# A two-layer trunk of convolution and attention on one NeuronCore: adding loads of half a weight piece, two woven projection blocks, an earlier turn

## The chip, the cores and the metric

The kernel runs on one core of a Trainium2 chip. The metric is the device time of one execution in microseconds; smaller is better. Before the change three runs took 1907.27 to 1909.2 us, with a median of 1909.15 us.

## The reference

Two layers work on 256 tokens of 2048 channels in float32. What matters of a layer:

```python
h = rmsnorm(x, norm_g)
proj = h @ w_in          # c_a, c_glu, c_gate, q_down, kv_down, k_pe, m_gate, g_conv, g_mla
...
y_conv = conv_branch(c_a, c_glu, c_gate, ...) @ w_proj_conv
y_mla = mla_branch(q_down, kv_down, k_pe, m_gate, ...) @ w_proj_mla
y = jax.nn.sigmoid(g_conv) * y_conv + jax.nn.sigmoid(g_mla) * y_mla
return x + y @ w_out
```

The conv branch is a gated unit, a causal depthwise convolution of width 31, a layer norm over the channels, a swish and a gate. The other branch is multi-head latent attention.

## The kernel before

**Products.** All weights stream from HBM once for each layer. A weight matrix is cut into blocks of 512 columns, and a block into pieces of two K tiles (`KS = 2`): 128 partitions by 2 x 512 columns, 512 KB. The projections with 2048 inputs (`gmla`, `gconv`, `pmla`, `pconv`, `wout` among them) have eight pieces to a block. To keep float32 accuracy each operand is split in two: `hi`, rounded to the type in which TensorE works, and `lo`, the remainder. A piece gives 12 matmuls: for two halves of the tokens and two K tiles, `hi` weights with the `hi` and the `lo` of the stationary side, and `lo` weights with its `hi`. One piece of one block is one tick of the program's clock; the text calls it a slot too.

**Splitting.** `split_hi` makes `hi` on ScalarE (ACT), `split_lo` makes `lo = raw - hi` on VectorE (DVE). `prepare`, called ahead of each unit's matmuls, splits `hi` three units ahead and `lo` two; both have four buffers. For the pieces listed in `ADDED_BY_DMA` DVE does nothing: ACT writes `lo = -hi` for both K tiles, and a DMA on the GpSimd (POOL) queue adds the raw weights to it from HBM. These are pieces 1 and 5 of the blocks of `gmla`, `gconv`, `pmla` and of the first two of `pconv` (where the first two pieces of a block are replaced, as told next, only piece 5).

**Seven in place of eight.** `gconv`, `wout` and the second half of `pconv` run as pairs of blocks (`SEVEN`). The first two pieces of both blocks of a pair are replaced by seven products of a quarter each (`q1` to `q7`, six matmuls each) on sums of weights and of activations. `q1`, `q7`, `q6` and `q5` stand in the tail of the block before (`TAIL`, counted from its end), the other three at the front of the pair. DVE forms the sums of weights (`sum`), `make_forms` those of the stationary side (`form_a`, `form_b`).

**Order.** `InOrder` keeps the instructions of each engine in the order in which the program writes them. Steps are put down for a slot to come (`at_slot`). What is left of DVE's time in a slot by `background`'s costs is filled from a queue, `fill`: first the taps of the convolution, then the layer norm and the gating (`layernorm`). The last step of these, `separated`, writes a quarter of `ycT` (512 channels), hi on ACT and lo on DVE. `pconv` reads it: pieces 0 and 1 use the first quarter, 2 and 3 the second, 4 and 5 the third, 6 and 7 the last. `before_pconv` puts in whatever is still missing of a quarter when a piece needs it.

**Turning.** An evacuated tile of `y` (or of the next layer's `h`) is turned by way of HBM: `park` writes it there in four DMAs, `fetch` reads it back after `fetch_at` slots, and after `at` slots DVE transposes within blocks of 32. `turn4` sets these numbers for each quarter `c`.

Every recorded operation has the line of `InOrder`'s helper, 132 (133 in the changed kernel), so instructions are known by their tiles: `acc`, `left`, `right` are PSUM accumulators, `tap` and `v_t` belong to the convolution, `turned` to a turn.

Of the kernel before, what the change touches and what calls it, by code (L numbers as in the profile page):

```python
# [11 lines left out]
F32 = mybir.dt.float32  # L12
# [108 lines left out]
def trunk(ctx: ExitStack, tc: tile.TileContext, xT, x, g_in, pos, win, wuq, wukv, wpc, wpm, wo, cst, rows, invf, out):  # L121
# [67 lines left out]

    TAIL = {8: (-7, -5, -3, -2), 12: (-7, -5, -3, -2)}  # L190

    def plan_all():
        blocks = [(l, k, i, pieces_of(l, s)) for l in range(DEPTH) for k, i, s in order_of_layer()]
        seven, home = None, 0
        for at, (l, k, i, block) in enumerate(blocks):
            first = (l, k, i) in SEVEN
            if at > 0 and blocks[at - 1][:3] in SEVEN:
                continue
# [8 lines left out]
            after = at + 1 + first  # L207
            following = blocks[after] if after < len(blocks) else None
# [76 lines left out]
    def split_hi(i):  # L285
        if i >= len(units) or i in highs:
            return
        load(i)
        form(i)
        n = units[i].n  # L290
        paired = n == PAIRED
        both = split_p.tile([P, KS, 2 * n if paired else n], F32R, tag="hi", name=f"hi{i}", bufs=4)
        highs[i] = both[:, :, :n]
        if paired:
            pairs_of[i] = both
        singly = i < N_SINGLE
        if i == 0:
            one = [slice(a, a + 1) for a in range(KS)]
            scale_x(0, "hi", vec)
            scale_x(0, "lo", vec)  # L300
            act.copy(highs[i][:, one[0]], full(i)[:, one[0]])
            scale_x(1, "hi", vec)
            act.copy(highs[i][:, one[1]], full(i)[:, one[1]])
            split_lo(i, one[0])
            scale_x(1, "lo", vec)
            split_lo(i, one[1])
        for a in () if i == 0 else range(0, KS, 1 if singly else KS):
            k = slice(a, a + 1 if singly else KS)

            if singly:  # L310
                act.copy(highs[i][:, k], full(i)[:, k])
            for c in range(min(i * KS + k.start, NCT), min(i * KS + k.stop, NCT)):
                scale_x(c, "hi", act)
                scale_x(c, "lo", vec)
            if singly:
                split_lo(i, k)
            else:
                act.copy(highs[i][:, k], full(i)[:, k])
        if units[i].added:
            lo = split_p.tile([P, KS, n], F32R, tag="lo", name=f"lo{i}", bufs=4)  # L320
            act.activation(lo, highs[i].bitcast(F32), AF.Copy, scale=-1.0)
            gps.dma_start(lo, sources[units[i].source][0], accum_op=ALU.add)
            done[i] = highs[i], lo, KS
        for a in range(1, LOAD_AHEAD + 1):
            load(i + a)

    def split_lo(i, k=slice(0, KS)):
        if i >= len(units) or done.get(i, (0, 0, 0))[2] >= k.stop:
            return
        n = units[i].n  # L330
        if i in pairs_of:
            lo = pairs_of[i][:, :, n:]
# [3 lines left out]
        done[i] = highs[i], lo, k.stop  # L336

# [27 lines left out]
    def background(n, more):  # L365
# [186 lines left out]
    def product(planned, stat, evacuate, evac_at=EVAC_AT, costs=(0.0, 0.0), before=None, tardy=None, closing=None):  # L552
# [4 lines left out]
        else:  # L557
            dst = [accumulators(f"acc{planned.pieces[0]}")]

        def evac(right, ts=range(T)):  # L560
            for t in ts:
                evacuate(*((right,) if seven else ()), t, dst[right][t][:, : 2 * n] if n == PAIRED else dst[right][t][:, :n])

# [6 lines left out]
        for at, tick in enumerate(planned.ticks):  # L570
# [16 lines left out]
            for t, kk, part in [(t, kk, p) for t in range(T) for p in range(2) for kk in range(KS)] if n == PAIRED else ():  # L587
# [4 lines left out]
                )  # L592
            for t, kk, part in () if n == PAIRED else order_of_products(i, final, j == tardy):
                k = j * KS + kk
# [6 lines left out]
                )  # L601
            if final and planned.begins:
                half = tuple(c / 2 for c in costs)
# [208 lines left out]
    for l in range(DEPTH):  # L812
# [711 lines left out]
        def evac_of(f, i, pl):  # L1524
            return (lambda b, t, ps: f(i + b, t, ps)) if pl.seven else (lambda t, ps: f(i, t, ps))

# [5 lines left out]
        for at_block, (kind, i, pl) in enumerate(planned):  # L1532
# [5 lines left out]
            def stage_behind(b):  # L1538
                return planned[b + 1 + bool(planned[b][2].seven)][0]

# [3 lines left out]

            of, after = pl.begins, at_block + 1 + bool(pl.seven)
            if of:
# [59 lines left out]
            elif kind == "pconv":  # L1606
                while "yc" not in keep:
                    run_fill()
                product(pl, stat_of(*keep["yc"]), evac_of(pconv_evac, i, pl), 0 if i + bool(pl.seven) == 3 else EVAC_AT, (2.4, 0.0),
                        before=before_pconv if i == 0 else None)  # L1610
# [118 lines left out]
```

## Time and profile before

| | |
|---|---|
| median of three runs | 1909.15 us |
| the profiled execution | 1904.81 us |
| its span, first to last instruction | 1903.0 us |
| mean granted TensorE clock | 0.995 |
| busy: TensorE, VectorE, ScalarE, GpSimd | 1874.6, 1664.4, 1407.1, 538.3 us |
| moved by DMA | 475.45 MB, 250 GB/s |

The views used are the page, the waits of an engine, the groups of instructions by form, the DMA issues, the timeline of one engine, and sums over stretches of time. In the waits a row names who waited, for what, and the microseconds in total, the number of times and the longest. In a timeline row stand the start, the length, the instructions, and in brackets the idle time before with what ended it. The gate stages (`gmla`, `gconv`) lie at about 500 to 685 us in the first layer and 1450 to 1630 in the second, `pmla` behind them, then `pconv` at about 778 to 835 and 1722 to 1785.

### The profile page before, as it was taken

How to read it: one execution, taken by the hardware profiler on the slowest of the kernel's cores; microseconds unless marked ns; L12 is line 12 of the kernel's file. 1: busy time of each engine (PE TensorE's matmuls, PEld its weight loads, DVE VectorE, ACT ScalarE, POOL GpSimd, SP SyncE). 2: the span in 40 equal slices, each digit the busy share in tenths (PEclk: the TensorE clock that was granted, in tenths of full speed). 3: DMA queues.
4: the chain of work that ended last, by engine and by line, in shares of the span. 5: the costliest groups of instructions: out<-in, count | busy, mean ns of one | idle time of the engine just before them, and what ended most of it. 6: DMA issues, size and time to landing. Idle time of an engine off the chain costs nothing. (4 is left out here: it accounts for less than half of the span.)

```text
span 1903.0 us, 26913 instructions
## 1 busy us (share of the span) xinstructions
PE 1874.6 (99%) x8389; PEld 1550.1 (81%) x8389; DVE 1664.4 (87%) x2618; ACT 1407.1 (74%) x2461; POOL 538.3 (28%) x990
## 2 busy tenths in 40 slices
PE   9999999999998999999999999999999989999999
PEld 8888888888877788788888888888887877887887
DVE  6998988889998898979869989888899988888895
ACT  6678888888886685755657689888899866776553
POOL 0155555532200000121421545555322000111211
PEclk9999999999999999999999999999999999999999
DMA  8777777787877689778976777787778867888785
GB/s 319 226 264 262 261 258 247 264 258 245 261 222 208 209 234 265 238 248 257 339 259 212 266 260 257 252 259 260 248 249 266 231 204 220 261 250 254 238 267 199
DMA packets 147312, 475.45 MB, mean 250 GB/s; under 512 B 24608, under 2 KB 29984, under 8 KB 147168
## 3 DMA queue, kind: packets, MB, share of 16 engines
q1 hardware_dynamic: 106416, 364.74, 57.7%
q0 software_dynamic: 39744, 107.79, 20.5%
q8 instruction: 66, 1.08, 0.2%
q10 hardware_dynamic: 1008, 1.20, 0.2%
q14 instruction: 78, 0.64, 0.1%
HBM read 429.59 MB, written 44.04 MB: 249 GB/s over the span
## 5 line engine op out<-in xcount | busy, mean ns | idle before, releaser
L132 ACT CAST hi<-raw 128x1024 fp32r<-128x1024 f32 (+2 forms) x683 | 697.2, 1028 | 325.7 <-PE acc L132 159.0
L132 DVE TENSOR_TENSOR lo<-raw,hi 128x1024 fp32r<-128x1024 f32 (+2 forms) x619 | 741.4, 1202 | 90.7 <-ACT hi L132 66.5
L132 PE MATMUL acc<-hi,hT 128*128 128x512 f32 (+1 forms) x1472 | 357.8, 384 | 0.0
L132 PEld LDWEIGHTS acc<-hi,hT 128*128 128x128 f32 x1472 | 271.5, 188 | 53.6
L132 PE MATMUL acc<-hi,h_hi 128*128 128x512 f32 (+1 forms) x736 | 225.6, 388 | 0.0
L132 PE MATMUL acc<-hi,h_lo 128*128 128x512 f32 (+2 forms) x736 | 221.3, 382 | 0.0
L132 DVE SCALAR_TENSOR_TENSOR v_t<-u_t,cst,v_t 128x256 f32<-128x256 f32 x508 | 215.8, 479 | 2.3
L132 ACT ACTIVATE tap<-u_t,cst 128x256 f32<-128x256 f32 x452 | 197.1, 499 | 4.4 <-DVE v_t L132 4.4
L132 PE MATMUL acc<-lo,h_hi 128*128 128x512 f32 (+1 forms) x704 | 191.2, 388 | 6.9 <-DMA lo<-in_win 6.9
L132 PE MATMUL acc<-lo,hT 128*128 128x512 f32 (+1 forms) x704 | 190.6, 388 | 5.4 <-DMA lo<-in_win 5.4
L132 DVE TENSOR_TENSOR v_t<-v_t,tap 128x512 f32<-128x512 f32 x226 | 155.4, 687 | 9.5 <-ACT tap L132 1.5
L132 PEld LDWEIGHTS acc<-hi,h_lo 128*128 128x128 f32 x736 | 138.1, 189 | 28.2
L132 PEld LDWEIGHTS acc<-lo,h_hi 128*128 128x128 f32 x704 | 131.2, 188 | 34.9 <-DMA lo<-in_win 8.6
L132 PEld LDWEIGHTS acc<-lo,hT 128*128 128x128 f32 x704 | 131.2, 188 | 33.4 <-DMA lo<-in_win 7.3
L132 PEld LDWEIGHTS acc<-hi,h_hi 128*128 128x128 f32 x736 | 136.7, 189 | 26.0
L132 POOL DMA_DIRECT2D turn_d<-gate x184 | 100.7, 556 | 187.7 <-ACT gate L132 96.4
L132 PE MATMUL acc<-hi,oT 128*128 128x512 f32 x512 | 127.8, 389 | 0.0
L132 PE MATMUL acc<-hi,qkc 128*128 128x512 f32 x448 | 115.4, 389 | 0.0
L132 PEld LDWEIGHTS acc<-hi,oT 128*128 128x128 f32 x512 | 95.8, 188 | 19.8
L132 POOL DMA_DIRECT2D lo<-in_win x24 | 21.2, 882 | 316.7 <-ACT lo L132 280.4
L132 POOL DMA_DIRECT2D turn_d<-su x128 | 70.1, 555 | 98.0 <-DVE su L132 89.1
L132 PEld LDWEIGHTS acc<-hi,qkc 128*128 128x128 f32 x448 | 83.6, 188 | 17.0
(265 smaller groups left out, 3013.7 us busy)
## 6 DMA issues: line engine op xcount, KB each, us to landing
raw<-in_win SPq DMA_DIRECT2D x401, 512.0 KB, 4.5
raw<-in_wo SPq DMA_DIRECT2D x68, 512.0 KB, 4.9
raw<-in_wpc SPq DMA_DIRECT2D x66, 512.0 KB, 4.6
raw<-in_wpm SPq DMA_DIRECT2D x64, 512.0 KB, 4.7
raw<-in_wukv SPq DMA_DIRECT2D x32, 512.0 KB, 4.2
turned<-turn_d POOLq DMA_DIRECT2D x56, 256.0 KB, 6.0
raw<-in_wuq SPq DMA_DIRECT2D x24, 512.0 KB, 4.3
turn_d<-qk POOLq DMA_DIRECT2D x128, 96.0 KB, 3.7
```

Source lines behind the costliest of these rows:

```text
L132: ins = getattr(self.engine, name)(*a, **k)
```

## The change

It has three parts. First, the pieces with an adding load become 0, 2, 4 and 6 in place of 1 and 5, and only the second K tile of the piece is made in that way: ACT negates 128x512, the DMA loads 256 KB, and DVE subtracts the first K tile. In such a piece the products with `lo` of the second K tile are put last. Second, the first two blocks of `pconv` are woven: six pieces of the first, two of the second, the last two of the first, six of the second. They are one block of 16 slots with two pairs of accumulators; the quarter products of the pair behind them keep their distance from its end. Third, the first quarter of `y` (and of `h`) is fetched after 3 slots and turned after 6, in place of 4 and 8.

```diff
-ADDED_BY_DMA = {(kind, i): (1, 5) for kind, blocks in (("gmla", 4), ("gconv", 4), ("pmla", 4), ("pconv", 2)) for i in range(blocks)}
+WOVEN = {(l, "pconv", 0): [(j, 0) for j in range(6)] + [(0, 1), (1, 1), (6, 0), (7, 0)] + [(j, 1) for j in range(2, 8)] for l in range(DEPTH)}
+ADDED_BY_DMA = {(kind, i): (0, 2, 4, 6) for kind, blocks in (("gmla", 4), ("gconv", 4), ("pmla", 4), ("pconv", 2)) for i in range(blocks)}
...
-    TAIL = {8: (-7, -5, -3, -2), 12: (-7, -5, -3, -2)}
+    TAIL = {8: (-7, -5, -3, -2), 12: (-7, -5, -3, -2), 16: (-7, -5, -3, -2)}
...
-            lo = split_p.tile([P, KS, n], F32R, tag="lo", name=f"lo{i}", bufs=4)
-            act.activation(lo, highs[i].bitcast(F32), AF.Copy, scale=-1.0)
-            gps.dma_start(lo, sources[units[i].source][0], accum_op=ALU.add)
-            done[i] = highs[i], lo, KS
+            lo, half = split_p.tile([P, KS, n], F32R, tag="lo", name=f"lo{i}", bufs=4), slice(KS - 1, KS)
+            act.activation(lo[:, half], highs[i][:, half].bitcast(F32), AF.Copy, scale=-1.0)
+            gps.dma_start(lo[:, half], sources[units[i].source][0][:, half], accum_op=ALU.add)
+            done[i] = highs[i], lo, 0
...
+        if units[i].added:
+            k = slice(0, KS - 1)
...
-            times += units[own].added * (1 if e == "act" else -1)
+            times += units[own].added * (0.5 if e == "act" else -0.5)
...
-            dst = [accumulators(f"acc{planned.pieces[0]}")]
+            dst = [accumulators(f"acc{planned.pieces[0]}_{b}") for b in range(1 + planned.twin)]
...
-            for t, kk, part in () if n == PAIRED else order_of_products(i, final, j == tardy):
+            order = [] if n == PAIRED else order_of_products(i, final, j == tardy)
+            if units[i].added and not final:
+                order.sort(key=lambda e: (e[2] == 2) * (1 + e[1]))
+            for t, kk, part in order:
...
-            if final and planned.begins:
+            if final and planned.begins and (seven or at == len(planned.ticks) - 1):
...
-                soon_at = dict(fetch_at=3, at=6) if c == 2 else {}
+                soon_at = {} if c == 1 else dict(fetch_at=3, at=6)
```

The first place is ScalarE in the last `gmla` block of the first layer, where the quarter products of the pair behind it stand. `hi211` and `hi213` are the splits of the quarter products `q6` and `q5`, `hi210`, `hi212` and `hi214` those of the block's pieces 4, 5 and 6. Before:

```order
L132 CAST hi210_6222<-raw208_6134 128x1024
L132 ACTIVATE tap_6243<-u_t_2564,cst_160 128x256 x2
L132 CAST hi211_6248<-sum208_6160 128x1024
L132 CAST hi212_6260<-raw209_6183 128x1024
L132 ACTIVATE lo212_6262<-hi212_6260 128x1024
L132 ACTIVATE tap_6280<-u_t_2564,cst_160 128x256 x2
L132 ACTIVATE tap_6283<-u_t_2564,cst_160 128x256 x2
L132 CAST hi213_6286<-raw220_6077 128x1024
```

The same stretch after the change:

```order
L133 CAST hi210_6239<-raw208_6149 128x1024
L133 ACTIVATE lo210_6241<-hi210_6239 128x512
L133 ACTIVATE tap_6265<-u_t_2564,cst_160 128x256 x2
L133 CAST hi211_6269<-sum208_6180 128x1024
L133 CAST hi212_6281<-raw209_6204 128x1024
L133 ACTIVATE tap_6298<-u_t_2564,cst_160 128x256 x2
L133 ACTIVATE tap_6301<-u_t_2564,cst_160 128x256 x2
L133 CAST hi213_6306<-raw220_6097 128x1024
L133 ACTIVATE tap_6324<-u_t_2564,cst_160 128x256 x2
L133 CAST hi214_6329<-raw210_6244 128x1024
L133 ACTIVATE lo214_6331<-hi214_6329 128x512
```

The negation has moved from piece 5, right behind the copy that waits for DVE's sum, to pieces 4 and 6, and is half as wide.

The second place is TensorE in the first `pconv` block of the first layer. `hi287` is its piece 5, and `ycT0` and `ycT1` are hi and lo of the conv branch's result. Before, piece 6 (`hi288`) follows in the same accumulators:

```order
L132 MATMUL acc276_0_7895<-lo287_7946,ycT0_7832 128x512 x2
L132 MATMUL acc276_1_7896<-lo287_7946,ycT0_7832 128x512 x2
L132 MATMUL acc276_0_7895<-hi288_7972,ycT0_7832 128x512 x2
L132 MATMUL acc276_0_7895<-hi288_7972,ycT1_7833 128x512 x2
L132 MATMUL acc276_1_7896<-hi288_7972,ycT0_7832 128x512 x2
L132 MATMUL acc276_1_7896<-hi288_7972,ycT1_7833 128x512 x2
```

After the change:

```order
L133 MATMUL acc276_0_0_7957<-lo287_8033,ycT0_7901 128x512 x2
L133 MATMUL acc276_0_1_7958<-lo287_8033,ycT0_7901 128x512 x2
L133 MATMUL acc276_1_0_7959<-hi288_8035,ycT0_7901 128x512 x2
L133 MATMUL acc276_1_0_7959<-hi288_8035,ycT1_7902 128x512 x2
L133 MATMUL acc276_1_1_7960<-hi288_8035,ycT0_7901 128x512 x2
L133 MATMUL acc276_1_1_7960<-hi288_8035,ycT1_7902 128x512 x2
```

Unit 288 is now the first piece of the second block, in the accumulators `acc276_1`, and uses the first quarter of `ycT`; the first block's piece 6 has become unit 290.

The third place is VectorE at the same time: from the remainder of piece 4 (unit 286) to the third quarter of `ycT`, which piece 4 uses. Before:

```order
L132 TENSOR_TENSOR lo286_7942<-raw280_7813,hi286_7923 128x1024
L132 TENSOR_TENSOR v_t_5584<-turned_7828,v_t_5584 128x2x128
L132 TENSOR_TENSOR v_t_5991<-turned_7828,v_t_5991 128x2x128
L132 STREAM_TRANSPOSE turned_7830<-turned_7830 128x512
L132 TENSOR_TENSOR v_t_5584<-turned_7830,v_t_5584 128x2x128
L132 TENSOR_TENSOR v_t_5991<-turned_7830,v_t_5991 128x2x128
L132 TENSOR_TENSOR ycT1_7833<-v_t_5584,ycT0_7832 128x512
```

After the change:

```order
L133 TENSOR_TENSOR lo286_7990<-raw280_7887,hi286_7988 128x512
L133 TENSOR_TENSOR v_t_6583<-v_t_6583,ln_stats_4145 128x2x256
L133 TENSOR_TENSOR v_t_7095<-v_t_7095,ln_stats_4145 128x2x256
L133 STREAM_TRANSPOSE turned_7876<-turned_7876 128x512
L133 TENSOR_TENSOR v_t_5608<-turned_7876,v_t_5608 128x2x128
L133 TENSOR_TENSOR v_t_6026<-turned_7876,v_t_6026 128x2x128
L133 TENSOR_TENSOR lo287_8033<-raw281_7910,hi287_8012 128x1024
L133 STREAM_TRANSPOSE turned_7878<-turned_7878 128x512
L133 TENSOR_TENSOR v_t_5608<-turned_7878,v_t_5608 128x2x128
L133 TENSOR_TENSOR v_t_6026<-turned_7878,v_t_6026 128x2x128
L133 TENSOR_TENSOR lo288_8037<-raw284_7935,hi288_8035 128x512
L133 TENSOR_TENSOR ycT1_7902<-v_t_5608,ycT0_7901 128x512
```

Two remainders, of units 287 and 288, have come in ahead of the third quarter, and its gating begins later in the row.

More of the change, by code (lines that the diff above doesn't have):

```diff
@@ L196, in plan_all @@
             first = (l, k, i) in SEVEN
-            if at > 0 and blocks[at - 1][:3] in SEVEN:
+            woven = WOVEN.get((l, k, i))
+            if at > 0 and (blocks[at - 1][:3] in SEVEN or blocks[at - 1][:3] in WOVEN):
                 continue
@@ L206, in plan_all @@
                     js.sort(key=lambda e: e[0] // 2)
-            after = at + 1 + first
+            block.twin = bool(first or woven)
+            js = woven or js
+            after = at + 1 + block.twin
             following = blocks[after] if after < len(blocks) else None
@@ L335, in split_lo @@
         vec.tensor_sub(lo[:, k], full(i)[:, k], highs[i][:, k].bitcast(F32))
-        done[i] = highs[i], lo, k.stop
+        done[i] = highs[i], lo, KS if units[i].added else k.stop
     steps, clock, late, early = [], [0], [], []
@@ L557, in product @@
         else:
-            dst = [accumulators(f"acc{planned.pieces[0]}")]
+            dst = [accumulators(f"acc{planned.pieces[0]}_{b}") for b in range(1 + planned.twin)]
         def evac(right, ts=range(T)):
             for t in ts:
-                evacuate(*((right,) if seven else ()), t, dst[right][t][:, : 2 * n] if n == PAIRED else dst[right][t][:, :n])
+                evacuate(*((right,) if planned.twin else ()), t, dst[right][t][:, : 2 * n] if n == PAIRED else dst[right][t][:, :n])
         if seven and seven.home:
@@ L1524, in evac_of @@
         def evac_of(f, i, pl):
[L1525 removed]
+            return (lambda b, t, ps: f(i + b, t, ps)) if pl.twin else (lambda t, ps: f(i, t, ps))
         uses_h = stat_of(h_hi, h_lo)
@@ L1538, in stage_behind @@
             def stage_behind(b):
-                return planned[b + 1 + bool(planned[b][2].seven)][0]
+                return planned[b + 1 + planned[b][2].twin][0]
             def forms_at(b):
@@ L1543, in forms_at @@
                 return ticks + TAIL[ticks][1] - (5 if ticks == 8 else 4)
-            of, after = pl.begins, at_block + 1 + bool(pl.seven)
+            of, after = pl.begins, at_block + 1 + pl.twin
             if of:
@@ L1608, in trunk @@
                     run_fill()
-                product(pl, stat_of(*keep["yc"]), evac_of(pconv_evac, i, pl), 0 if i + bool(pl.seven) == 3 else EVAC_AT, (2.4, 0.0),
+                product(pl, stat_of(*keep["yc"]), evac_of(pconv_evac, i, pl), 0 if i + pl.twin == 3 else EVAC_AT, (2.4, 0.0),
                         before=before_pconv if i == 0 else None)
```

## The prediction

> **What bounds the kernel.** I read the page first. TensorE (PE) is busy almost all the time, so only what makes PE wait, or lowers its clock, can move the end.
>
> ```profile
> PE 1874.6 (99%) x8389; PEld 1550.1 (81%) x8389; DVE 1664.4 (87%) x2618; ACT 1407.1 (74%) x2461; POOL 538.3 (28%) x990
> ```
>
> Then the waits of PE's weight loads, which show what each pause ended on (us in total, times, longest):
>
> ```profile
> PEld acc L132 <- DMA lo<-in_win: 15.9, 9, 5.0
> PEld right L132 <- DMA lo<-in_win: 5.4, 2, 2.8
> PEld left L132 <- DMA lo<-in_win: 3.7, 4, 1.3
> PEld acc L132 <- ACT ycT L132: 3.0, 2, 2.4
> PEld acc L132 <- DMA lo<-in_wpc: 2.4, 3, 1.0
> PEld acc L132 <- DMA lo<-in_wpm: 2.3, 5, 0.8
> PEld acc L132 <- DVE ycT L132: 1.5, 2, 1.1
> ```
>
> Nearly every pause inside the program belongs to the two things that the change edits: the remainder `lo` that is made by an adding load (29.7 us in five rows) and the conv branch's turned result `ycT` (4.5 us in two). A pause can cost more than its length, so I next counted matmuls by stretch. In each row the first x is the number of matmuls, and the number behind the DVE, ACT and POOL columns is the granted PE clock.
>
> ```profile
> 500.00:700.00 200.00, 189.53 (x807) 153.43 (x806) 178.81 (x267) 149.24 (x226) 16.96 (x23) 0.97 0.76 225
> 750.00:850.00 100.00, 96.88 (x415) 77.98 (x414) 85.68 (x124) 63.46 (x78) 18.71 (x30) 0.98 0.82 244
> 850.00:950.00 100.00, 100.00 (x439) 82.22 (x438) 88.74 (x105) 57.97 (x79) 27.93 (x51) 1.00 0.87 294
> 1450.00:1600.00 150.00, 141.59 (x603) 114.38 (x602) 135.58 (x197) 110.55 (x168) 13.49 (x19) 0.98 0.76 227
> 1700.00:1800.00 100.00, 98.84 (x432) 80.47 (x431) 84.44 (x112) 63.29 (x79) 18.30 (x30) 1.00 0.84 253
> 590.00:594.70 4.70, 0.11 (x1) 0.00 (x0) 3.57 (x5) 3.86 (x6) 0.00 (x0) 0.90 0.99 260
> 594.70:601.00 6.30, 6.29 (x16) 4.95 (x17) 3.28 (x5) 1.53 (x2) 0.00 (x0) 0.53 0.52 170
> ```
>
> The stretch 850 to 950 has no pause: 439 matmuls in 100 us, 0.228 us each. At that pace the other four would hold 877, 439, 658 and 439, and they hold 807, 415, 603 and 432: missing are 70, 24, 55 and 7, or 16.0, 5.5, 12.5 and 1.6 us, 35.6 in all. The last two rows show why this exceeds the bare waits: after 4.7 us without work the clock is 0.53 for the next 6.3 us. In the 5.5 us of the stretch 750 to 850 the waits on `ycT` are the bulk; I put 4.5 on them. That leaves 31 us for the adding loads.
>
> **Term 1: the adding loads.** One late load of before, in the order ACT, POOL, PE:
>
> ```profile
> 582.99 1.05 ACT L132 CAST hi<-sum 128x1024 fp32r<-128x1024 f32 x1 [3.92 <-DVE sum L132]
> 583.95 1.05 ACT L132 CAST hi<-raw 128x1024 fp32r<-128x1024 f32 x1
> 585.02 1.06 ACT L132 ACTIVATE lo<-hi 128x1024 fp32r<-128x1024 f32 x1
> 586.38 0.87 POOL L132 DMA_DIRECT2D lo<-in_win  x1 [16.32 <-ACT lo L132]
> 594.71 2.08 PE L132 MATMUL acc<-lo,h_hi 128*128 128x512 f32 x4 [4.60 <-DMA lo<-in_win]
> ```
>
> From the start of the `hi` copy to the first use of `lo` are 10.76 us: copy 1.05, negation 1.06, 0.3 to the issue, the rest the transfer. PE wanted the remainder at 594.71 - 4.60 = 590.1. The copy had itself started late, behind a copy of a sum that waited 3.92 us for DVE. The same chain at a place where ACT was on time:
>
> ```profile
> 608.74 1.06 ACT L132 CAST hi<-raw 128x1024 fp32r<-128x1024 f32 x1 [0.63 <-ACT ym L132]
> 609.83 1.06 ACT L132 ACTIVATE lo<-hi 128x1024 fp32r<-128x1024 f32 x1
> 618.78 1.20 PE L132 MATMUL left<-lo,h_hi 128*128 128x512 f32 x4 [0.60 <-DMA lo<-in_win]
> ```
>
> Chain 10.04 us, wanted after 618.78 - 0.60 - 608.74 = 9.44. So a chain of ten to eleven microseconds meets an allowance of nine and a half: that is the systematic stall of the gate stages. The allowance is fixed by the four `hi` buffers (the copy for a unit can start when PE has finished the unit four before it) and it shrinks by 1.4 us, six matmuls, for each quarter product that stands in place of a whole piece.
>
> The changed chain: copy 1.05, negation of half the width, then the transfer of 256 KB instead of 512 KB. The rows that price it (groups by form, DMA issues with KB and median us to landing, and the spread of the adding loads):
>
> ```profile
> L132 ACT CAST hi<-raw 128x512 fp32r<-128x512 f32 x22 | 13.5, 618 | 7.2 <-DMA raw<-in_win 3.1 <-PE acc L132 2.5 <-DVE hi L132 0.7
> raw<-in_win SPq DMA_DIRECT2D x401, 512.0 KB, 4.5
> raw<-in_win SPq DMA_DIRECT2D x22, 256.0 KB, 3.0
> lo<-in_win POOLq DMA_DIRECT2D x24, 512.0 KB, 7.8
> x_dram<-xres POOLq DMA_DIRECT2D x8, 256.0 KB, 5.9
> turned<-turn_d POOLq DMA_DIRECT2D x56, 256.0 KB, 6.0
> DMA to landing us min/median/max: 5.5/7.8/9.3
> ```
>
> The negation takes 0.62. No row shows an adding load of 256 KB. Its lower bound is 7.8 x 3.0/4.5 = 5.2 us, as plain loads shrink; its upper bound is 7.8, no shrinking. I take 6.0, since POOL's own plain transfers of 256 KB take 5.9 and 6.0. The chain is then 1.05 + 0.62 + 0.3 + 6.0 = 8.0 us. The allowance grows, because the order of products puts the loaded half's two matmuls last: two matmuls later, 0.45 us, so 9.9. A margin of 1.9 where there was a deficit.
>
> Here the Trainium skill speaks against halving. Its page "DMA: Bandwidth & Descriptors", section on the anatomy of a DMA on the gpsimd path, fits one DMA as about 2.0 us plus its bytes over 436 thousand per us: 3.2 us for 512 KB and 2.6 for 256. The trace's 7.8 for the former is far above that, and by the rule the half load would save only 0.6 us, landing after 7.2; the chain would be 9.2 and still inside 9.9.
>
> How many units stand where? Of the 52 adding loads in each layer I count 37 with three whole pieces ahead (allowance about 11), 12 with one quarter product among them (9.9), and 3 with two (8.5: piece 6 in the last `gmla` block, in the second block of the first `gconv` pair and in the second woven block, where `q6` and `q5` stand next to it). At 8.0 all are covered if ACT is on time. The row at 583.95 shows it 3 us late at just such a place, so I leave 0.7 us on each of the six tight units in both layers, 4 us. Term 1: 31 - 4 = **27 us** gained. Bounds: 31 if nothing remains; below, the rivals.
>
> **What the other engines do for it.** DVE gives up 48 whole remainders and 104 halves, and ACT's negations go from 48 whole to 104 half ones:
>
> ```profile
> L132 DVE TENSOR_TENSOR lo<-raw,hi 128x1024 fp32r<-128x1024 f32 x597 | 724.2, 1217 | 85.0 <-ACT hi L132 65.7 <-DMA raw<-in_win 6.2 <-PE acc L132 6.2
> L132 DVE TENSOR_TENSOR ycT<-v_t,ycT 128x512 fp32r<-128x512 f32 x16 | 10.3, 687 | 5.3 <-ACT ycT L132 5.3
> L132 ACT ACTIVATE lo<-hi 128x1024 fp32r<-128x1024 f32 x48 | 51.0, 1063 | 5.5 <-PE acc L132 4.0
> ```
>
> With 0.687 us for a DVE subtraction of half width, before saves 48 x 1.217 = 58 us of DVE, after saves 104 x (1.217 - 0.687) = 55. ACT goes from 51 to 104 x 0.62 = 64. Both are spread over 1900 us, and neither engine is the bound. POOL issues 56 more DMAs of at most 0.9 us each and is 28% busy; what could stand ahead of a load on its in-order queue is a fetch of a turned tile or the parking of a gate, and in the rows above the load left 0.3 us after its negation. Cost taken: 0.
>
> **Term 2: the woven blocks.** In the first layer PE met the conv branch's last quarter too early:
>
> ```profile
> 797.13 1.14 ACT L132 CAST ycT<-v_t 128x512 fp32r<-128x512 f32 x2 [1.09 <-DVE v_t L132]
> 798.43 1.29 DVE L132 TENSOR_TENSOR ycT<-v_t,ycT 128x512 fp32r<-128x512 f32 x2
> 797.80 0.73 PE L132 MATMUL acc<-hi,ycT 128*128 128x512 f32 x2 [1.99 <-ACT ycT L132]
> 799.17 2.93 PE L132 MATMUL acc<-hi,ycT 128*128 128x512 f32 x6 [0.63 <-DVE ycT L132]
> 789.80 2.38 PE L132 MATMUL acc<-hi,ycT 128*128 128x512 f32 x8
> ```
>
> With two pieces of the second block ahead of it (24 matmuls, 5.5 us), PE gets there at 795.8 + 5.5 = 801.3 on this clock, and the quarter is whole at 798.43 + 1.29 = 799.7: that stall goes. The third quarter is not moved. At 789.80 its eight matmuls already took 2.38 us, 0.4 too long, and the new DVE order puts more ahead of it: two whole and three half subtractions (4.5 us) where three whole ones stood (3.65). PE also comes sooner against DVE, since its own stalls are gone. I put 2.5 us there (between 0.4 as now, and about 4, if the late quarter's price moves to it whole). Term 2: 4.5 - 2.5 = **2 us**. The second layer shows almost no such wait and gets none.
>
> **Term 3: the first quarter turned sooner.** One slot less to the fetch and two to the turn, three slots (8.2 us) for a fetch that lands in 6.0. The third quarter is turned on this timetable already, and DVE's waits for turned tiles are few:
>
> ```profile
> DVE turned L132 <- DMA turned<-turn_d: 7.5, 4, 3.4
> ```
>
> It only gives back the two slots by which weaving delays the first evacuation. 0, at worst one wait of 3.4.
>
> **The sum.** 27 + 2 + 0 = 29 us. The profiled execution took 1904.81 (span 1903.0 and 1.8 around it), 4.3 below the median of 1909.15. 1909 - 29 = **1880 us**.
>
> **Rivals.** *The half load lands no sooner* (7.8): what is fixed in an adding load may be most of it. Chain 9.8: the 24 units at 9.9 stall when ACT is at all late, say 0.3, the six tight ones by 1.3 + 0.7: 7 + 12 = 19 us remain. Gain 31 - 19 + 2 = 14, 1895 us. For it: no row of a smaller adding load. Against it: plain loads do shrink. Chance 0.14. By the skill's 7.2 it would lie between this and my forecast.
>
> *DVE becomes the bound.* In the gate stage of the first layer it works 178.8 of 200 us; without PE's 16 lost us that is 97%, and sums and remainders may come late in place of the loads. Against it is a stretch in which both run so full:
>
> ```profile
> 450.00:500.00 50.00, 50.00 (x225) 41.52 (x224) 48.74 (x64) 45.03 (x81) 11.93 (x21) 1.00 0.78 253
> ```
>
> If half of term 1 turns into DVE waits, the gain is 15: 1894 us. Chance 0.12.
>
> *Slower: 104 loads in place of 48 get into each other's way.* They now come every second piece, 5.5 us apart, shorter than one landing, so two are often in flight beside the loads of raw weights. With a chain c the stalls sum to 74 x (c - 11) + 24 x (c - 9.9) + 6 x (c - 8.5), each bracket where positive. They reach today's 31 at c = 10.6, a landing of 8.6 us; at 9.0 they are 26 + 15 = 41, so 41 - 31 - 2 = 8 us slower, 1917. The slowest load of before took 9.3, so it can be, but every load would have to be so. Chance 0.06. A change that does next to nothing (landing at the break-even, or a hidden gain): 0.04.
>
> **Numbers.** My forecast 0.64. The range runs from 1869 (all 35.6 us gone from the 1904.8 of the profiled execution) to 1897, which takes in the first two rivals. Two runs of this kernel differ by about 0.2%, which is what a measurement can tell. Faster by more: 0.64 + 0.14 + 0.12 = 0.90; same 0.04; slower 0.06.
>
> **What would show it.** The changed profile should have adding loads of 256 KB landing in about 6 us; PE's waits on `lo` under a fifth of 29.7; the stretches of the gate stages at a clock of 1.00; one wait on `ycT` left near the third quarter in the first layer, none at the last. I am wrong if the loads land after 8 us or more, if PE's waits name DVE's `lo` or `sum`, or if the `ycT` wait is more than 5 us.

## The result, and the profile after

The changed kernel takes 1879.85 us (median of 4 runs, 1878.11 to 1888.48), the kernel before 1908.28 on the same chip (4 runs, 1907.27 to 1909.2). The ratio is 0.986, with a 95% interval of 0.983 to 0.989. The profiled executions took 1904.81 and 1880.02, 24.8 us apart where the medians are 28.4 apart. One execution among the later runs, of the kernel with whole-width loads, took 2326 us at a granted clock of 0.75 where its three others took 1937 to 1943; it is left out everywhere.

The busy times in the page of the changed kernel:

```profile
PE 1865.2 (99%) x8389; PEld 1546.7 (82%) x8389; DVE 1661.4 (88%) x2669; ACT 1418.7 (76%) x2511; POOL 587.5 (31%) x1046
```

PE has the same 8389 matmuls and is busy 9.4 us less, since fewer of them ran at the lower clock; the other 15 us of the gain are time in which it stood still.

The waits of PE's weight loads after the change (us in total, times, longest):

```profile
PEld acc L133 <- DMA lo<-in_win: 5.1, 4, 2.9
PEld right L133 <- DVE lo L133: 2.1, 3, 1.0
PEld acc L133 <- ACT ycT L133: 2.0, 1, 2.0
PEld acc L133 <- DMA lo<-in_wpc: 1.3, 1, 1.3
PEld left L133 <- DMA lo<-in_win: 0.7, 2, 0.4
PEld acc L133 <- DVE ycT L133: 0.4, 1, 0.4
PEld right L133 <- DMA lo<-in_win: 0.3, 1, 0.3
```

The waits on the adding loads have fallen from 29.7 us in five rows to 5.1 + 1.3 + 0.7 + 0.3 = 7.4, and those on `ycT` from 4.5 to 2.4. The same stages in windows of the same length, moved 5 to 20 us earlier, since the program runs ahead of its old times (PE's count is the first x, the granted clock stands behind POOL):

```profile
495.00:695.00 200.00, 197.03 (x857) 161.40 (x856) 189.37 (x304) 161.47 (x255) 33.95 (x43) 0.99 0.85 245
745.00:845.00 100.00, 97.47 (x419) 79.32 (x419) 86.88 (x127) 63.60 (x83) 22.18 (x34) 0.98 0.81 245
1435.00:1585.00 150.00, 148.54 (x653) 122.00 (x652) 144.66 (x224) 123.31 (x193) 25.82 (x33) 1.00 0.86 247
1680.00:1780.00 100.00, 100.00 (x441) 82.45 (x440) 86.11 (x118) 62.90 (x79) 23.80 (x37) 1.00 0.84 259
```

At the pace of the undisturbed stretch of before (877, 439, 658 and 439 matmuls) these are short of 20, 20, 5 and none, at 0.228 us each 4.6 + 4.6 + 1.1 + 0 = 10.3 us. Before it was 35.6. The difference, 25.3, agrees with the gain of the span (1903.0 - 1878.2 = 24.8). A count of this kind is good to two or three matmuls a stretch (the last one holds 441 where the pace gives 439), some 2 us in all; within that, nothing of the gain came from elsewhere. The gains by stage are 11.4, 0.9, 11.4 and 1.6.

The time that the new load takes, from the DMA issues (KB, median us to landing):

```profile
lo<-in_win POOLq DMA_DIRECT2D x56, 256.0 KB, 6.0
lo<-in_wpm POOLq DMA_DIRECT2D x32, 256.0 KB, 6.4
lo<-in_wpc POOLq DMA_DIRECT2D x16, 256.0 KB, 6.0
```

And the spread of all 104, from the view of the tile:

```profile
DMA to landing us min/median/max: 3.6/6.1/7.8
```

Half the bytes land in 6.1 us where the whole took 7.8.

### The profile page after: what moved, and what is told of

The parts are those of the page before. It is cut to its first block, busy times and chain, and to the rows that moved or that the text cites. A ratio compares the mean times of both kernels' runs of the same rounds, so it can differ in the third digit from the quotient of the medians.

```text
span 1878.2 us, 27286 instructions
## 1 busy us (share of the span) xinstructions
PE 1865.2 (99%) x8389; PEld 1546.7 (82%) x8389; DVE 1661.4 (88%) x2669; ACT 1418.7 (76%) x2511; POOL 587.5 (31%) x1046
## 3 DMA queue, kind: packets, MB, share of 16 engines
q8 instruction: 66, 1.08, 0.2%
## 4 chain that ended last, share of the span: by engine, by line
PE 90%; DVE 4%; DMA 3%; issue 2%; ACT 1%; POOL 0%; DVEq 0%; POOLq 0%; ACTq 0%
PE acc L133 68%; PE left L133 10%; PE right L133 10%; DVE v_t L133 2%; DVE lo L133 1%; PE o_ps L133 1%; PE s1w L133 1%; DMA raw<-in_win 1%; DMA lo<-in_win 1%; PE s L133 1%; ACT hi L133 0%; DVE sum L133 0%; DMA raw<-in_wo 0%; DMA lo<-in_wpc 0%; DMA turned<-turn_d 0%
## 5 line engine op out<-in xcount | busy, mean ns | idle before, releaser
L133 ACT CAST hi<-raw 128x1024 fp32r<-128x1024 f32 (+2 forms) x683 | 697.0, 1028 | 287.4 <-PE acc L133 159.9
L133 DVE TENSOR_TENSOR lo<-raw,hi 128x1024 fp32r<-128x1024 f32 (+2 forms) x667 | 742.6, 1120 | 69.7 <-ACT hi L133 54.1
L133 PE MATMUL acc<-hi,hT 128*128 128x512 f32 (+1 forms) x1472 | 358.1, 384 | 0.3 <-ACT hT L133 0.3
L133 PEld LDWEIGHTS acc<-hi,hT 128*128 128x128 f32 x1472 | 271.4, 188 | 54.4 <-ACT hT L133 0.7
L133 PE MATMUL acc<-hi,h_hi 128*128 128x512 f32 (+1 forms) x736 | 225.4, 388 | 0.0
L133 DVE SCALAR_TENSOR_TENSOR v_t<-u_t,cst,v_t 128x256 f32<-128x256 f32 x514 | 219.8, 479 | 2.9
L133 PE MATMUL acc<-hi,h_lo 128*128 128x512 f32 (+2 forms) x736 | 220.9, 381 | 0.0
L133 ACT ACTIVATE tap<-u_t,cst 128x256 f32<-128x256 f32 x446 | 195.4, 498 | 4.4 <-DVE v_t L133 4.4
L133 PE MATMUL acc<-lo,h_hi 128*128 128x512 f32 (+1 forms) x704 | 190.0, 386 | 2.4 <-DMA lo<-in_win 2.4
L133 PE MATMUL acc<-lo,hT 128*128 128x512 f32 (+1 forms) x704 | 189.7, 386 | 1.5 <-DMA lo<-in_win 1.5
L133 PEld LDWEIGHTS acc<-hi,h_lo 128*128 128x128 f32 x736 | 137.9, 188 | 28.0
L133 DVE TENSOR_TENSOR v_t<-v_t,tap 128x512 f32<-128x512 f32 x223 | 153.2, 687 | 5.9
L133 PEld LDWEIGHTS acc<-hi,h_hi 128*128 128x128 f32 x736 | 136.6, 189 | 25.9
L133 POOL DMA_DIRECT2D turn_d<-gate x184 | 100.7, 565 | 174.3 <-ACT gate L133 91.8
L133 PEld LDWEIGHTS acc<-lo,h_hi 128*128 128x128 f32 x704 | 131.1, 188 | 29.0 <-DMA lo<-in_win 2.9
L133 PEld LDWEIGHTS acc<-lo,hT 128*128 128x128 f32 x704 | 130.8, 188 | 28.5 <-DMA lo<-in_win 2.3
L133 POOL DMA_DIRECT2D lo<-in_win x56 | 49.2, 879 | 280.5 <-ACT lo L133 200.9
L133 PE MATMUL acc<-hi,oT 128*128 128x512 f32 x512 | 127.8, 389 | 0.0
L133 PE MATMUL acc<-hi,qkc 128*128 128x512 f32 x448 | 115.4, 389 | 0.0
L133 PEld LDWEIGHTS acc<-hi,oT 128*128 128x128 f32 x512 | 95.8, 188 | 19.7
L133 POOL DMA_DIRECT2D turn_d<-su x128 | 69.8, 553 | 98.5 <-DVE su L133 91.8
L133 PEld LDWEIGHTS acc<-hi,qkc 128*128 128x128 f32 x448 | 83.6, 188 | 17.0
```

Of the source, the lines that this page charges most:

```text
L133: ins = getattr(self.engine, name)(*a, **k)
```

## The experiments

The twelve runs were made on three other chips; each ratio is to runs of the kernel before on that same chip. There the kernel before had medians of 1903.11, 1903.46 and 1904.91 us, so a bare time of one experiment is compared only with kernels on its own chip. Some two thousandths, about 4 us, is what a ratio of these runs can tell.

### Which of the three parts gives the gain

**The loads alone** (the woven blocks and the earlier turn undone):

```diff
-WOVEN = {(l, "pconv", 0): [(j, 0) for j in range(6)] + [(0, 1), (1, 1), (6, 0), (7, 0)] + [(j, 1) for j in range(2, 8)] for l in range(DEPTH)}
+WOVEN = {}
...
-                soon_at = {} if c == 1 else dict(fetch_at=3, at=6)
+                soon_at = dict(fetch_at=3, at=6) if c == 2 else {}
```

> The changed kernel with its first part alone: half-width adding loads, no woven blocks, first quarter turned as before. By the forecast's terms the loads are nearly all of the gain: about 24 us off the time before (1884 us), with the stall of the last ycT quarter back at 3 to 5 us in the first layer. The rival, that the weave is what pays, expects over 1900.

Measured: 1878.8 us (1877.6 to 1880.19), ratio 0.987 (0.985 to 0.989): as good as the whole change. The 24 us that I expected came; the stall of the last quarter of `ycT` did not come back at 3 to 5 us, PE waits 0.74 us for it. Three windows of this kernel:

```profile
745.00:845.00 100.00, 97.65 (x419) 79.06 (x418) 86.43 (x123) 63.49 (x82) 22.23 (x34) 0.98 0.80 243
770.00:790.00 20.00, 17.65 (x68) 13.13 (x67) 18.42 (x33) 12.32 (x19) 2.23 (x3) 0.91 0.81 240
800.00:812.00 12.00, 12.00 (x54) 9.80 (x53) 8.16 (x9) 6.15 (x7) 2.85 (x4) 1.00 1.00 342
```

And the two short ones of the changed kernel:

```profile
770.00:790.00 20.00, 18.39 (x73) 14.45 (x72) 18.32 (x30) 13.17 (x20) 2.67 (x3) 0.91 0.82 250
800.00:812.00 12.00, 11.08 (x49) 8.74 (x48) 8.52 (x12) 7.36 (x8) 6.57 (x11) 1.00 0.94 307
```

Over the 100 us of the conv projection both kernels do 419 matmuls. Weaving wins five of them at 770 to 790, where the quarters of `ycT` come in, and loses five at 800 to 812, where the second woven block waits for an adding load. Its worth beside the new loads is nothing that these runs can tell. The wait for the third quarter of `ycT` is there without the weave too:

```profile
777.54 2.77 PE L133 MATMUL acc<-hi,ycT 128*128 128x512 f32 x8 [1.61 <-ACT ycT L133]
```

The changed kernel has the same 1.61 us at that product (779.03, shown further on). So it is not the weave that makes this wait: PE, without its own stalls, comes sooner.

**The weave and the earlier turn alone**, on the old whole-width loads of pieces 1 and 5:

```diff
+WOVEN = {(l, "pconv", 0): [(j, 0) for j in range(6)] + [(0, 1), (1, 1), (6, 0), (7, 0)] + [(j, 1) for j in range(2, 8)] for l in range(DEPTH)}
 ADDED_BY_DMA = {(kind, i): (1, 5) for kind, blocks in (("gmla", 4), ("gconv", 4), ("pmla", 4), ("pconv", 2)) for i in range(blocks)}
...
+                soon_at = {} if c == 1 else dict(fetch_at=3, at=6)
```

> The woven blocks and the earlier turn on whole-width adding loads at pieces 1 and 5. By the forecast's second term 2 to 5 us are gained (1903 to 1907), with PE's waits on lo as long as before, about 30 us in the weight loads. The rival, that weaving moves the wait from the last to the third quarter and gains nothing, expects 1908 and an ycT wait of some 2 us at another place.

Measured: 1908.31 us (10 runs, 1905.73 to 1912.97) against 1903.11 (19 runs), ratio 1.0028 (1.0015 to 1.0040). Alone, these two parts cost 5 us. PE's wait on the loads of the conv projection, and its longest place, in the order POOL, ACT, POOL, PE:

```profile
PEld acc L133 <- DMA lo<-in_wpc: 7.4, 5, 3.4
```

```profile
810.21 4.42 POOL L133 DMA_DIRECT2D turn_d<-gate  x8 [18.53 <-DVE gate L133]
811.95 1.06 ACT L133 ACTIVATE lo<-hi 128x1024 fp32r<-128x1024 f32 x1
814.62 0.98 POOL L133 DMA_DIRECT2D lo<-in_wpc  x1
822.94 1.19 PE L133 MATMUL acc<-lo,ycT 128*128 128x512 f32 x4 [2.94 <-DMA lo<-in_wpc]
```

No wait on `ycT` stands among the ten longest any more, but `in_wpc` has gone from 2.4 to 7.4 us. The weave evacuates the first block two slots later, and the eight DMAs that park its gate now go out of POOL's queue just when this load is ready: the negation ends at 813.01, the load is issued 1.6 us later, and PE waits 2.94. In the second layer the parking stands in the same place (1757.47 to 1761.87), the load is issued 1.0 us late and PE waits 1.08. In the kernel before, the same load left 0.3 us after its negation. That is the largest part of what can be located: this profile is 2.2 us longer than that of before, and where the rest of the 5 us goes is not shown. My expectation held neither for the forecast nor for the rival that I named; neither had this wait in it.

**The earlier turn alone**, on the kernel before:

```diff
-                soon_at = dict(fetch_at=3, at=6) if c == 2 else {}
+                soon_at = {} if c == 1 else dict(fetch_at=3, at=6)
```

> The kernel before with the earlier turn of the first quarter alone. The forecast's third term: no change, 1908 us within 3 us either way; the rival is a DVE wait for the turned tile, up to 3.4 us slower.

Measured: 1905.77 us (10 runs), ratio 1.0009 (0.9998 to 1.0020). DVE's waits for turned tiles, 7.5 us before:

```profile
DVE turned L132 <- DMA turned<-turn_d: 8.8, 5, 3.7
```

1.3 us more idle time on DVE and no effect on the end that could be told.

### Is it the size of the load, its place, or the order of products

**The new places with whole-width loads** (pieces 0, 2, 4 and 6, weave kept; the new order of products, which serves the half loads, is gone too):

```diff
-            lo, half = split_p.tile([P, KS, n], F32R, tag="lo", name=f"lo{i}", bufs=4), slice(KS - 1, KS)
-            act.activation(lo[:, half], highs[i][:, half].bitcast(F32), AF.Copy, scale=-1.0)
-            gps.dma_start(lo[:, half], sources[units[i].source][0][:, half], accum_op=ALU.add)
-            done[i] = highs[i], lo, 0
+            lo = split_p.tile([P, KS, n], F32R, tag="lo", name=f"lo{i}", bufs=4)
+            act.activation(lo, highs[i].bitcast(F32), AF.Copy, scale=-1.0)
+            gps.dma_start(lo, sources[units[i].source][0], accum_op=ALU.add)
+            done[i] = highs[i], lo, KS
```

> The changed kernel with the adding loads of whole width (128x1024, 512 KB, both K tiles) at the same pieces 0, 2, 4 and 6. If the size of the load is what shortened the chain, the chain is back at ten microseconds and met twice as often: slower than the changed kernel by 20 to 60 us, 1900 to 1940. If it was the place of the loads, or the work taken from DVE, it is as fast as the changed kernel, 1880. In the last gmla block the raw weights of piece 4 should be on time, since ACT and not DVE releases the raw buffers.

Measured: 1936.85 us (three runs, 1936.72 to 1943.37), ratio 1.0186 (1.0157 to 1.0215). The spread of the loads, PE's waits on them, and the load of piece 2 in the last `gmla` block, in the order ACT, ACT, POOL, PE:

```profile
DMA to landing us min/median/max: 5.2/8.2/10.9
```

```profile
PEld acc L133 <- DMA lo<-in_win: 22.8, 15, 3.4
PEld acc L133 <- DMA lo<-in_wpm: 18.2, 15, 3.5
PEld right L133 <- DMA lo<-in_win: 12.3, 8, 2.9
PEld left L133 <- DMA lo<-in_win: 10.8, 7, 2.8
PEld acc L133 <- DMA lo<-in_wpc: 7.2, 6, 1.6
```

```profile
574.56 1.06 ACT L133 CAST hi<-raw 128x1024 fp32r<-128x1024 f32 x1 [1.08 <-PE acc L133]
575.65 1.06 ACT L133 ACTIVATE lo<-hi 128x1024 fp32r<-128x1024 f32 x1
577.00 0.88 POOL L133 DMA_DIRECT2D lo<-in_win  x1 [7.74 <-ACT lo L133]
586.88 1.53 PE L133 MATMUL acc<-lo,h_hi 128*128 128x512 f32 x4 [2.69 <-DMA lo<-in_win]
```

The waits on `lo` are 71.3 us, ten times those of the changed kernel, and the loads themselves are slower than in the kernel before: median 8.2 for 7.8, slowest 10.9 for 9.3. That fits loads that crowd each other, though no run shows the crowding itself. The step from -1.3% to +1.9% is made by their width and the work on ACT and DVE that goes with it, at equal places and equal number (the order of products is worth some 4 us, by the next run). The prediction's formula for stalls has the right size but no more: with a chain of 1.06 + 1.06 + 0.47 + 8.2 = 10.8 and allowances 0.45 shorter without the new order, 74 x 0.25 + 24 x 1.35 + 6 x 2.75 = 67 us; with the 0.29 us from negation to issue of the rows above it gives 48, since 74 units stand just at the edge. The copy of piece 4, at 581.50, waited 0.74 us for PE and not for raw weights, as expected, and its remainder came in time (595.42, no wait).

**Without the new order of products** (all else as changed):

```diff
-            if units[i].added and not final:
-                order.sort(key=lambda e: (e[2] == 2) * (1 + e[1]))
```

> The changed kernel with the products in the old order: the two matmuls on the loaded half are not put last. By the forecast's working they are wanted up to 0.45 us earlier, inside the margin of most units: 0 to 4 us slower, 1880 to 1884, with a few more waits on lo. The rival, that the order carries the gain, expects more than 10 us slower.

Measured: 1883.42 us (1879.38 to 1888.82), ratio 0.9898 (0.9877 to 0.9919). Its waits on the adding loads are little changed: `in_win` has 5.4 us on `acc`, and `in_wpc` 3.1, 1.8 us more than in the changed kernel. A worth of up to 4 us for the 0.45 us that the order gives each load would fit, but the interval does not separate it from none.

**Half loads at the odd pieces:**

```diff
-ADDED_BY_DMA = {(kind, i): (0, 2, 4, 6) for kind, blocks in (("gmla", 4), ("gconv", 4), ("pmla", 4), ("pconv", 2)) for i in range(blocks)}
+ADDED_BY_DMA = {(kind, i): (1, 3, 5, 7) for kind, blocks in (("gmla", 4), ("gconv", 4), ("pmla", 4), ("pconv", 2)) for i in range(blocks)}
```

> The changed kernel with the half-width adding loads at pieces 1, 3, 5 and 7 instead of 0, 2, 4 and 6. If the size of the load decides and not its place, the time stays within 8 us of the changed kernel's 1880. It moves the loads away from piece 4 behind q7 to pieces 1, 3 and 5, the last behind q6, where the kernel before had its longest stall: if the place behind a sum decides, that stall comes back there in both layers, some 4 us each.

Measured: 1892.01 us (1889.92 to 1895.19), ratio 0.9943 (0.9925 to 0.9962): over half of the gain is gone, and the time is not within 8 us of the changed kernel. Nor does a stall come back at piece 5, since the loads hardly stall: all rows on `lo` together have 9.0 us, where the changed kernel has 7.4. The two longest of PE's waits:

```profile
PEld acc L133 <- ACT ycT L133: 9.4, 3, 3.8
PEld acc L133 <- DMA lo<-in_win: 3.5, 3, 1.6
```

PE meets three quarters of `ycT` too early. From 745 to 845 us this kernel does 381 matmuls where the changed one does 419, 38 x 0.228 = 8.7 us of the 9.9 by which their spans differ (1888.1 and 1878.2). The places do not act through the transfers here. The planner subtracts what each slot's remainders take from what DVE and ACT may be given besides, so another set of pieces is another order of the gating work on both. That this order makes the quarters late is my reading of the rows; no run kept the odd pieces with the old order. DVE was not full: a window of this stage has it busy 42.2 of 55 us (49.0 in the changed kernel), and in its row it stands idle ahead of the late quarter, waiting for ACT.

```profile
745.00:800.00 55.00, 46.88 (x190) 37.20 (x189) 42.21 (x73) 34.49 (x50) 9.24 (x12) 0.93 0.74 217
```

```profile
783.03 1.29 DVE L133 TENSOR_TENSOR ycT<-v_t,ycT 128x512 fp32r<-128x512 f32 x2 [2.32 <-ACT ycT L133]
```

### What is left, and whether it can be had

Two stalls of the changed kernel are the largest left. The first is piece 4 of the last `gmla` block in the first layer, with `q7` ahead of it, in the order ACT, ACT, POOL, PE:

```profile
576.49 1.06 ACT L133 CAST hi<-raw 128x1024 fp32r<-128x1024 f32 x1 [1.95 <-DMA raw<-in_win]
577.57 0.64 ACT L133 ACTIVATE lo<-hi 128x512 fp32r<-128x512 f32 x1
578.67 0.87 POOL L133 DMA_DIRECT2D lo<-in_win  x1 [9.44 <-ACT lo L133]
585.15 0.74 PE L133 MATMUL acc<-lo,h_hi 128*128 128x512 f32 x2 [2.43 <-DMA lo<-in_win]
```

From the copy to the use are 8.66 us, against the 8.0 that I had summed. But the copy itself began late, 1.95 us of it for raw weights. The wait is 2.43. The second is the third quarter of `ycT`, in the order ACT, DVE, PE, PE:

```profile
778.36 1.14 ACT L133 CAST ycT<-v_t 128x512 fp32r<-128x512 f32 x2
779.01 1.29 DVE L133 TENSOR_TENSOR ycT<-v_t,ycT 128x512 fp32r<-128x512 f32 x2
779.03 2.94 PE L133 MATMUL acc<-hi,ycT 128*128 128x512 f32 x8 [1.61 <-ACT ycT L133]
781.76 1.91 PE L133 MATMUL acc<-lo,ycT 128*128 128x512 f32 x4
```

**Weaving two pieces sooner**, so that PE gets to the third quarter later:

```diff
-WOVEN = {(l, "pconv", 0): [(j, 0) for j in range(6)] + [(0, 1), (1, 1), (6, 0), (7, 0)] + [(j, 1) for j in range(2, 8)] for l in range(DEPTH)}
+WOVEN = {(l, "pconv", 0): [(j, 0) for j in range(4)] + [(0, 1), (1, 1), (4, 0), (5, 0), (6, 0), (7, 0)] + [(j, 1) for j in range(2, 8)] for l in range(DEPTH)}
```

> The changed kernel with the second block's first two pieces put in after piece 3 of the first block instead of after piece 5, so that the third and the last quarter of ycT are both met two pieces later. If the wait left at the third quarter (1.61 us and the half clock behind it, 3.7 us in all) is DVE's being two slots behind, it goes: 3 to 4 us faster than the changed kernel, 1876. The rival is that the wait follows DVE to the last quarter, and nothing is gained.

Measured: 1880.77 us (6 runs, 1875.49 to 1882.24), ratio 0.9877 (0.9859 to 0.9896). The wait on `ycT` is gone from the list. Since the changed kernel had not run on this chip, both were run again on the third.

**The changed kernel again**, with no edit:

> The changed kernel itself, so that it can be compared on one chip with the three beside it: 0.985 to 0.989 of the time of before, with PE's waits at piece 4 of the last gmla block and at the third ycT quarter as in its first profile.

Measured: 1880.37 us (1879.01 to 1882.96), ratio 0.9875 (0.9858 to 0.9893), as expected. The same waits are there, but PE's on `lo` come to 6.2 + 1.5 + 1.2 + 0.4 = 9.3 us where the first profile had 7.4: so much they differ between executions of one kernel.

**The sooner weave again**, on the same chip as that:

> The earlier weave (second block's pieces after piece 3 instead of piece 5) beside the changed kernel on the same chip. By the theory that PE met the third quarter of ycT before DVE had it: 2 to 4 us faster than the changed kernel and no wait on ycT. The rival, that the time of a run is not set by these small waits: within 1 us.

Measured: 1878.61 us (1878.02 to 1879.7), ratio 0.9865 (0.9849 to 0.9881). The intervals overlap: a gain of 1.8 us is not shown. The 2.4 us on `ycT` are gone, and on `lo` PE waits 3.2 us at `left` and 3.1 for `in_wpc`, 1.7 and 1.9 more than in the changed kernel run beside it. The count says the same: from 745 to 845 us it does 429 matmuls where that one does 420, in the first gate stage (495 to 695) 852 where that one does 862. What the conv projection won, 2.1 us, the gate stage lost, 2.3, in this execution; the first run of the same edit had 861 there. Stalls that differ so much from run to run hide a gain of this size.

**No adding load at the late piece 4**, in the two blocks where it stalls:

```diff
+ADDED_BY_DMA.update({("gmla", 3): (0, 2, 6), ("pconv", 1): (0, 2, 6)})
```

> The changed kernel without adding loads at piece 4 of the last gmla block and of the second woven block: DVE makes those remainders whole. These are the units behind q7, at which PE still waits 2.43 and 1.62 us (gmla) and 0.9 (woven). By the theory that the raw weights come late there, held by DVE, and leave the adding load no time, the waits go and 5 to 7 us with them, 1874. The rival, by the forecast's working, is that the tight units are the pieces 6, which keep their loads: no change.

Measured: 1883.96 us (1882.55 to 1885.57), ratio 0.9899 (0.9881 to 0.9918). The stall at piece 4 went as it should, and the first gate stage does 872 matmuls in place of 857, 3.4 us won. But my expectation for the time failed, since from 745 to 845 us there are 387 in place of 419, 7.3 us lost. PE's longest waits (the added line makes L133 into L134):

```profile
PEld acc L134 <- ACT ycT L134: 8.6, 3, 3.5
PEld acc L134 <- ACT hi L134: 1.8, 3, 1.0
PEld right L134 <- ACT hi L134: 1.7, 1, 1.7
```

DVE takes back half a remainder in each of the two blocks, and the quarters of `ycT` are late again, as with the odd pieces.

**That load moved to piece 7**, so that DVE keeps the help:

```diff
+ADDED_BY_DMA.update({("gmla", 3): (0, 2, 6, 7), ("pconv", 1): (0, 2, 6, 7)})
```

> The changed kernel with the adding load of piece 4 moved to piece 7 in the last gmla block and in the second woven block, so that DVE keeps its share of the work. If the place behind q7 is what leaves an adding load no time, the waits at 582, 1521 and 808 us go and none comes in their place: 3 to 6 us faster than the changed kernel. If, as in the run without those loads, DVE's own order is what matters, waits on ycT or on DVE's sums take their place and nothing is gained.

Measured: 1880.89 us (1879.63 to 1882.26), ratio 0.9877 (0.9860 to 0.9893), the changed kernel's own, as the second half of my expectation had it. Other waits took the place of those that went, most of them at the pair of blocks behind (`right`, `left`):

```profile
PEld right L134 <- DVE lo L134: 3.1, 3, 2.1
PEld left L134 <- DMA lo<-in_win: 2.9, 4, 1.3
```

**Both, moved load and sooner weave** (the two edits above together):

> Both edits together on the changed kernel: 5 to 9 us faster than it if the two waits are independent, with under 10 us lost in all beside the start; no faster than the earlier weave alone if the rival holds.

Measured: 1879.08 us (5 runs, 1876.97 to 1883.63), ratio 0.9868 (0.9848 to 0.9888). No version beats the changed kernel by more than these runs can tell.

## Why the prediction was right, point by point

**The main mechanism held.** The forecast was 1880, the median 1879.85. The load's price was 6.0, with bounds of 5.2 and 7.8; measured 6.0 to 6.4. That the width decides at the new places is shown by the whole-width run (1.0186) beside the changed kernel (0.986). The places are not free either: half loads at the odd pieces stall hardly more and keep less than half of the gain. Half loads at the old pieces 1 and 5 were not run, so what the larger number alone is worth stays open. Here the fit of the Trainium skill's "DMA: Bandwidth & Descriptors", section on the anatomy of a DMA on the gpsimd path, comes, as an estimate, to 3.2 us for 512 KB and 2.6 for 256; the runs had 7.8 and 6.1, a saving of 1.7 us where the fit has 0.6. By rows of this kernel POOL's own transfers of the same size were the better guide.

**Term 1 was about right, for all that these runs can tell.** I had 27 us; the loads alone gave 24 (21 to 28 by the interval). Of the 31 us I left 4; 7.4 us of bare waits remained. The step that failed is where the rest would be: "piece 6" with two quarter products among the three pieces ahead. What remained stood at piece 4, two units behind `q7` (2.43 us at 585.15 in the first layer, 1.46 at 1522.91 in the second, 0.92 at 808.97 in the second woven block), with one quarter among them. I had assumed that ACT would be on time except behind a copy of DVE's sum; here it waited for raw weights. PE's 575 to 595 has 70 matmuls of a possible 88, so the first of these stalls cost 4.1 us with its clock. Why the raw weights are late can be read from the loads: one is issued at 569.96, 0.03 us after DVE's `sum` ends, and lands 6.4 us later, 0.1 before the copy of piece 4 starts. In the other two places the load is likewise issued right behind a `sum`, at 1507.66 and 793.83, takes 6.4 and 6.8, and lands within 0.2 us of the copy. So the buffer for this load seems to come free only with DVE's `sum`, and the load then takes longer than the median of 4.6 to 4.9 for raw weights. No run tried a `sum` made sooner or one more raw buffer.

**Term 2 was wrong.** I had 2 us for the weave. Beside the new loads it is nothing (419 matmuls with and without), and with whole loads the weave and the earlier turn make it 0.28% slower. The sizes that I worked out came true: the last quarter's stall went, and the third quarter's grew to about 3.4 us (15 matmuls missing in the window 770 to 790), where I had 2.5 and bounds of 0.4 to 4. But two steps failed. I booked both against the weave, and the loads alone do most of it: without the weave the third quarter has the same 1.61 us, and the last quarter's stall has shrunk to 0.74. And among the costs of the other engines I had named the parking of a gate as what could stand ahead of an adding load on POOL's queue, and taken 0 for it; with the weave and whole loads it stood there in both layers, at 2.94 and 1.08 us of PE's time.

**Term 3 was right**: 1.0009 (0.9998 to 1.0020). In the changed kernel DVE's waits for turned tiles rose to more than the one wait of 3.4 that I named, but no wait of PE names them:

```profile
DVE turned L133 <- DMA turned<-turn_d: 18.5, 8, 5.3
```

**The sum** was 29; the two profiled executions differ by 24.8, and the ratios of the repeat, 0.9858 to 0.9893, come to 20 to 27 us. That the time came out at 1879.85 owes something to the base: I took 29 from the median, 4.3 above the execution that the sum was made against. By the runs, terms 1 and 2 are worth some 24 us and nothing.

**The rivals.** The load that lands no sooner fell at once (6.1). The crowding loads fell for half loads (slowest 7.8) and came true for whole ones, at 35 us above the kernel before: a landing of 8.2 was past the break-even there, which I had put at 8.6 for half loads, since the negation is 0.43 longer and the allowance 0.45 shorter (8.6 - 0.88 = 7.7). DVE as the bound did not come, at 189.4 of 200 us busy in the first gate stage (95%). But one of my signs of being wrong did come, in small: PE's waits name DVE's `lo` in three rows, 2.1 + 1.0 + 0.4 = 3.5 us where there were 0.4. And the waits on the adding loads are a quarter of 29.7, not under a fifth. What the odd pieces and the missing fourth showed in its place is a rival that I had not named: with DVE at 42.2 of 55 us, another order of the small work on it and on ACT makes a result late.

## What to carry to other kernels

Price a transfer inside its chain: from the first copy that can start to the product that needs it, against the time that the buffers allow. When the chain is a microsecond too long, a systematic stall arises, and making each transfer smaller can remove it even at twice the number of transfers, if the bytes and not the issue make it long; measure both widths at equal places before believing in the places. Price, too, what shares a queue with the transfer: here the parking of a tile, moved by another edit, delayed a load. And when a helper's schedule is made by a planner, any edit of what it is charged reorders all its other work: look for the new wait on a result that the edit does not mention.

## What the runs showed of the hardware that was not expected

Short pauses of PE were enough for half speed right behind them: in the third quarter's row above 1.61 us, and in its weight loads, whose row follows, a further 0.43 us a moment later.

```profile
779.75 1.50 PEld L133 LDWEIGHTS acc<-hi,ycT 128*128 128x128 f32 x6 [0.43 <-DVE ycT L133]
```

The window of the changed kernel that holds the four matmuls at 781.76, which took 1.91 us:

```profile
781.50:784.50 3.00, 3.00 (x10) 2.36 (x9) 2.96 (x6) 1.68 (x2) 0.00 (x0) 0.58 0.24 75
```

The granted clock is 0.58 here. So a stall can cost more than its length: 2.0 us idle, and of the 88 matmuls that 20 us hold, the 73 of the window 770 to 790 leave 3.4 us missing. Not every pause does: behind the 1.46 us at 1522.91 the clock stays at 1.00 (window 1515 to 1530, 60 matmuls). The Trainium skill's "TensorE: Matmul & The Clock Gate", section "What's actually happening", puts the fall to half clock after at least one idle window of about 3.4 us; this trace shows it after less than two thirds of that, both pauses taken together.

The issue of an adding load takes POOL 0.87 us at 256 KB as at 512 KB, so the saving of 1.7 us lies wholly behind the issue. And the kernel before took 1908.28 us on the first chip and 1903 to 1905 on three others, 0.2 to 0.3% apart: as much as all the smaller effects here.
